# Two vector operations, four weight splits, one gate and one normalisation moved in a four-layer mixed-attention kernel

## The chip, the cores and the metric

The kernel runs on one core of one Trainium2 chip. The metric is the device time of one execution in microseconds (us), lower is better; before, it is the median of 3 runs.

## What is computed

The input is x, 512 tokens of 1024 channels in float32. Four residual layers follow each other: one of sliding-window attention (layer A), one of sparse attention with a compressed, a selected and a window branch (layer B), and two hybrid layers with three mixers side by side, a matrix LSTM, a gated linear attention and a sparse attention with top-k keys (layers C0 and C1). In short:

```python
def rms_norm(x, g):
    xf = x * lax.rsqrt(jnp.mean(x * x, axis=-1, keepdims=True) + EPS)
    return xf * g

def nsa_layer(x, norm_g, w_in, q_gain, w_out, table, k_cmp, v_cmp, k_slc, v_slc, k_win, v_win):
    proj = rms_norm(x, norm_g) @ w_in
    ...
    o_all = jnp.stack([o_cmp, o_slc, o_win], axis=2)
    o = jnp.einsum('bschd,bsch->bshd', o_all * jax.nn.silu(z), jax.nn.sigmoid(gate_logits))
    return x + o.reshape(B_, S, HQ) @ w_out

def hybrid_layer(x, norm_g, w_in, ..., w_out, rel_bias):
    p = split_columns(rmsnorm(x, norm_g) @ w_in)
    ...
    dq, dk = rmsnorm(p['dsa_q'], dsa_q_g), rmsnorm(p['dsa_k'], dsa_k_g)
    y = jnp.concatenate([y_ml, y_gla, y_dsa], axis=-1) @ w_out
    return x + y
```

So at each border between layers the new x is known only when the last output projection has been added to it, and the next layer's first product needs the norm of all 512 tokens.

## The kernel before, in words

**Layout.** x stays in SBUF as four token tiles (t = 0 to 3) of 128 tokens by 1024 channels. The normalised x is needed with channels on the partitions, so `norm_x` (L316) does for each tile: sums of squares on ScalarE (ACT, L301), a short chain of one-column VectorE (DVE) operations for the reciprocal root (L302, L139 to L149, three Newton steps of L145 and L149), the scaling `xs` on DVE in two halves of 512 channels (L326, or L328 with a gain row `E` that was fetched by the two transfers of L312), eight transposes on TensorE (PE, L331, four to a half, into a PSUM bank with the tag `t`), and `split_evac` (L359), which copies each bank out as a high part `xhi` (ACT, L361) and a rest `xlo` (DVE, L362).

**Weights.** Products keep float32 accuracy with three matmuls each: high times high (L264), rest times high (L265), high times rest (L266), or L284 to L286 with the operands swapped. `piece` (L220) streams a weight piece: a transfer from HBM into `wraw` (L228, on the queue of SyncE, SP; pieces that don't fill their tile are preceded by a memset on GpSimd, POOL, L225), the high part `whi` on ACT (L235, L242), the rest `wlo` partly on DVE (L238, L244) and partly on POOL (L249; L246 applies a gain first). The share of DVE is `dve_lo`: 0 in layer B's main part, 0.5 around its last projection, 1 in layers C. Below, mv0 is the first weight group of layer C0; its product is 96 matmuls.

**Order.** The program text gives an order, and a list scheduler with a cost model turns it once, at build time, into a fixed queue for each engine. An engine then runs its queue strictly in that order and waits at an instruction whose inputs or buffer are not ready. `s.after(a, b)` (L118) is a dependency written by hand that keeps `a` behind `b`. PSUM has 8 banks: in layer B the tags g, t, s, o have 2, 3, 2, 1 of them; in layers C 2, 2, 3, 1. Layer C's pool is opened when layer B's is closed, so its banks lie on those of layer B, in the order of first use.

**Places that matter here.** In `layer_b` the gain row `gk` is scaled on DVE (L818) and the tile `VBD` is cleared on DVE (L910). Attention is a loop over 4 head groups g and 4 token tiles t; each of the three branches (br) ends in `Block.gate` (L960): DVE writes the scaled branch `og` (L968), then POOL multiplies it by the gate `sz` (L972 for the first branch, L974 for the others) and adds it to `acc` (L975). After the third branch `to_T` (L353) transposes `acc` on PE, and `oT` goes to the output projection `out(g)`, whose sums are added to x on DVE (L586). Projections out(0) to out(2) are woven between later attention steps; out(3) stands at the end. Its last 12 matmuls, those of t = 3, need the very last gate. `layer_c` then calls `norm_x` and, in layer C0, `consts_c` (L1725), which loads and casts a mask (`gmask`, POOL, L1733) and makes small constants (DVE, L1735 to L1739). In both layers C `Dsa.early` loads two gain rows (L155) and scales one by the other on DVE (`dgk`, L1618).

Of the kernel before, what the change touches and what calls it, by code (L numbers as in the profile page):

```python
# [10 lines left out]
F32 = mybir.dt.float32  # L11
# [10 lines left out]
NT = 4  # L22
# [54 lines left out]
class Ctx:  # L77
# [281 lines left out]
    def split_evac(s, ps, hi, lo):  # L359
        nc = s.nc  # L360
        nc.scalar.activation(hi, ps, AF.Copy)  # L361
        nc.vector.tensor_tensor(lo, ps, hi.bitcast(F32), OP.subtract)  # L362

# [439 lines left out]
def layer_b(s):  # L803
    nc, tc, ia = s.nc, s.tc, s.ia
    outer = s.stack
    with ExitStack() as st:
# [3 lines left out]
        if not s.gains_known:  # L810
# [6 lines left out]
        gk = s.bcast_row(lp, ia["kv_k_gain"], 192, "gk")  # L817
        nc.vector.scalar_tensor_tensor(gk.rearrange("p (b d) -> p b d", d=64), gk.rearrange("p (b d) -> p b d", d=64), 0.125,  # L818
                                       gq[:, None, :].to_broadcast([P, 3, 64]), op0=OP.mult, op1=OP.mult)
        kvd = s.dram.tile([2, SEQ, 256], F32, name="kvd")  # L820
# [77 lines left out]
        rc = s.rstd(css, 1, 64, "rc")  # L898
        nc.vector.scalar_tensor_tensor(kc, kc, rc, gk[:, :64], op0=OP.mult, op1=OP.mult)
        s.k_pack(kc[:, None, :], kcT[:, None, :], wk, "s", "kcs")  # L900
# [3 lines left out]
        for g in range(4):  # L904
            hT4 = s.epage()[:, :256].rearrange("p (j a c) -> p j a c", j=2, a=4)
            for j in range(2):
                nc.scalar.copy(hT4[:, j], hT[:, j, None, 32 * g:32 * g + 32].to_broadcast([P, 4, 32]))
                nc.tensor.matmul(pc[:, g * 64:(g + 1) * 64], hT4[:, j].rearrange("p a c -> p (a c)"), w2t[:, j],
                                 start=j == 0, stop=j == 1)
        nc.vector.memset(VBD, 0.0)  # L910
        for j in range(4):
# [42 lines left out]
        class Block:  # L954
# [5 lines left out]
            def gate(self, po, den, br):  # L960

                g, t = self.g, self.t
                nc.vector.reciprocal(den, den)
                nc.vector.tensor_tensor(den, den, gt[:, t, br * 16 + 4 * g:br * 16 + 4 * g + 4], OP.mult)
                if br == 0 and t == 0:
                    nc.vector.memset(den[0:31], 0.0)
                og = s.opage()
                nc.vector.scalar_tensor_tensor(og.rearrange("p (h d) -> p h d", d=64), po.rearrange("p (h d) -> p h d", d=64),  # L968
                                               0.25, den[:, :, None].to_broadcast([P, 4, 64]), op0=OP.mult, op1=OP.mult)
                if br == 0:  # L970
                    self.acc = wk.tile([P, 256], F32, name="acc", tag="acc", bufs=2)
                    nc.gpsimd.tensor_tensor(self.acc, og, groups[g][1][br][t], OP.mult)  # L972
                else:
                    nc.gpsimd.tensor_tensor(og, og, groups[g][1][br][t], OP.mult)  # L974
                    nc.gpsimd.tensor_tensor(self.acc, self.acc, og, OP.add)  # L975

# [119 lines left out]

        def out(g):
            yield from s.w_out_slices(s.w(f"o{g}"), lambda k, t: (outs[g, t][:, 0, k], outs[g, t][:, 1, k]))

# [3 lines left out]
        s.pipeline(steps, fill)  # L1103
        s.dve_lo = 0.5
        for _ in out(3):
            pass
    s.stack = outer

# [84 lines left out]
def layer_c(s, L):  # L1193
    nc, tc, ia = s.nc, s.tc, s.ia
    outer = s.stack
    with ExitStack() as st:
# [5 lines left out]
        s.pens = s.pool(f"pens{L}", 3)  # L1202
        s.norm_x(ia["norm_g_2"][L])
        if L == 0:
            consts_c(s)
        k = type("K", (), {})()
# [5 lines left out]
        for e, fill in events():  # L1212
            if e in ROWS:
                tasks["m", ROWS[e]].row()
            if e[0] == "top_keys":

                s.behind = top_keys(s, k), e[1]
            elif e[0] == "keys_known":
                for _ in s.behind[0] if s.behind else []:
                    pass  # L1220
                s.behind = None
            else:
                s.weave(run(e), [(UNITS[f[0], f[1][0]], run(f)) for f in fill])
    s.stack = outer

# [380 lines left out]
class Dsa:  # L1606
# [5 lines left out]
    def early(self):  # L1612
        s, k, p = self.s, self.k, self.p
        nc, ia = s.nc, s.ia
        if p == 0:
            gq = s.bcast_row(k.lp, ia["dsa_q_g_2"][k.L], P, "dgq")
            k.dgk = s.bcast_row(k.lp, ia["dsa_k_g_2"][k.L], P, "dgk")
            nc.vector.scalar_tensor_tensor(k.dgk, k.dgk, P ** -0.5, gq, op0=OP.mult, op1=OP.mult)  # L1618
        wts = s.w(f"dq{p}")
# [167 lines left out]
```

## Time and profile before

| | |
|---|---|
| median of 3 runs | 2055.94 us (2050.4 to 2060.71) |
| profiled execution, its own time | 2054.46 us |
| profiled execution, span of the trace | 2052.7 us |
| PE busy | 1970.0 us, 96% of the span |
| DVE busy | 1415.8 us, 69% |
| ACT busy | 907.7 us, 44% |
| POOL busy | 637.6 us, 31% |
| mean granted TensorE clock | 0.990 of full speed |
| chain of work that ended last | PE 61%, DVE 15%, DMA 2%, issue 2%, ACT 2%, POOL 1% |

The span runs from the first to the last instruction; 1.76 us of the execution lie around it. PE is busy nearly always, so only those places count where PE stands or runs at half clock: what is moved elsewhere costs nothing. Times of single rows are counted from the start of the span.

### The profile page before, as it was taken

The page shows a single profiled execution, that of the slowest core. Times are in us where ns is not written, and L with a number is a line of the kernel's source. Part 1 is how long each engine was busy: PE and PEld are TensorE (multiplying, and loading weights), DVE is VectorE, ACT ScalarE, POOL GpSimd, SP SyncE. Part 2 cuts the span into 40 slices and gives each one's busy share as a digit, 9 for nine tenths or more (in the row PEclk, how much of TensorE's full clock was granted, in tenths as well). Part 3 has the DMA queues.
Part 4 walks back from the last instruction along what each step waited for, and adds up shares of the span by engine and source line. Part 5 has one row for each costly group of instructions (what it writes and reads, how often), then busy time and mean ns, then how long its engine had stood idle before and what let it go on. Part 6 is the DMA issues. An engine that isn't in the chain of part 4 may idle for free.

```text
span 2052.7 us, 29949 instructions
## 1 busy us (share of the span) xinstructions
PE 1970.0 (96%) x10139; PEld 1636.9 (80%) x10139; DVE 1415.8 (69%) x3901; ACT 907.7 (44%) x2113; POOL 637.6 (31%) x684
## 2 busy tenths in 40 slices
PE   7999989999999988999899999999999989999999
PEld 6788877788888877777778888887877778888887
DVE  6467749645656675689958775557589967965564
ACT  4355435445444553544433343434555333433432
POOL 3444325454535331015333220211013443321111
PEclk9999999999999998999999999999999999999999
DMA  5321233321121101322232232223313232332231
GB/s 178 108 82 55 82 104 108 103 83 52 55 59 60 44 9 51 109 86 72 66 103 78 74 97 87 83 78 84 108 43 99 61 94 62 95 100 84 67 107 43
DMA packets 158966, 164.93 MB, mean 80 GB/s; under 512 B 26137, under 2 KB 132560, under 8 KB 158812
## 3 DMA queue, kind: packets, MB, share of 16 engines
q1 hardware_dynamic: 158812, 163.01, 26.8%
q8 instruction: 80, 1.31, 0.3%
q14 instruction: 74, 0.61, 0.1%
HBM read 157.17 MB, written 5.80 MB: 79 GB/s over the span
## 4 chain that ended last, share of the span: by engine, by line
PE 61%; DVE 15%; DMA 2%; issue 2%; ACT 2%; POOL 1%; SPq 0%; DVEq 0%; ACTq 0%; POOLq 0%
PE b_g L264 12%; PE b_g L266 12%; PE b_g L265 12%; PE b_g L284 4%; PE b_g L285 4%; PE b_g L286 4%; DVE wlo L238 3%; PE b_o L1076 3%; PE b_s L1046 2%; DVE topw L1336 1%; PE b_t L1069 1%; PE b_s L1307 1%; DVE m L1335 1%; DVE x L586 1%; ACT whi L235 1%
## 5 line engine op out<-in xcount | busy, mean ns | idle before, releaser
L264 PE MATMUL b_g<-whi,xhi 128*128 128x512 f32 x1280 | 510.2, 399 | 21.0 <-DVE my L1525 14.2
L266 PE MATMUL b_g<-whi,xlo 128*128 128x512 f32 x1280 | 507.2, 397 | 4.2 <-DVE xlo L362 4.2
L265 PE MATMUL b_g<-wlo,xhi 128*128 128x512 f32 x1280 | 508.2, 397 | 0.1
L235 ACT ACTIVATE whi<-wraw 128x1024 fp32r<-128x1024 f32 (+2 forms) x250 | 261.0, 1047 | 181.5 <-PE b_g L266 100.0
L238 DVE TENSOR_TENSOR wlo<-wraw,whi 128x512 fp32r<-128x512 f32 (+2 forms) x376 | 268.5, 756 | 69.8 <-ACT whi L235 68.0
L264 PEld LDWEIGHTS b_g<-whi,xhi 128*128 128x128 f32 x1280 | 242.9, 190 | 75.1 <-issue 13.4
L266 PEld LDWEIGHTS b_g<-whi,xlo 128*128 128x128 f32 x1280 | 243.0, 190 | 54.4 <-DVE xlo L362 6.1
L265 PEld LDWEIGHTS b_g<-wlo,xhi 128*128 128x128 f32 x1280 | 243.1, 190 | 48.5 <-POOL wlo L249 0.9
L249 POOL TENSOR_TENSOR wlo<-wraw,whi 128x512 fp32r<-128x512 f32 (+1 forms) x138 | 182.2, 1345 | 90.7 <-ACT whi L235 81.9
L284 PE MATMUL b_g<-xhi,whi 128*128 128x512 f32 x400 | 160.7, 402 | 6.8 <-DVE x L586 4.6
L285 PE MATMUL b_g<-xlo,whi 128*128 128x512 f32 x400 | 157.9, 395 | 0.0
L286 PE MATMUL b_g<-xhi,wlo 128*128 128x512 f32 x400 | 157.6, 394 | 0.0
L586 DVE TENSOR_TENSOR x<-x,b_g 128x512 f32<-128x512 f32 x192 | 130.1, 681 | 37.4 <-PE b_g L266 36.4
L1531 POOL TENSOR_TENSOR mT<-my,mT 128x512 fp32r<-128x512 f32 x32 | 42.9, 1347 | 247.1 <-PE b_s L1307 160.3
L284 PEld LDWEIGHTS b_g<-xhi,whi 128*128 128x128 f32 x400 | 75.1, 188 | 27.1 <-DVE x L586 7.1
L1076 PEld LDWEIGHTS b_o<-v,PT 128*128 128x128 f32 x640 | 85.3, 198 | 6.3 <-DVE PT L1072 1.1
L286 PEld LDWEIGHTS b_g<-xhi,wlo 128*128 128x128 f32 x400 | 75.1, 188 | 16.4 <-issue 1.2
L285 PEld LDWEIGHTS b_g<-xlo,whi 128*128 128x128 f32 x400 | 75.2, 188 | 16.3 <-issue 1.2
L1525 DVE SCALAR_TENSOR_TENSOR my<-b_g,vec,my 128x511 f32<-128x511 f32 (+2 forms) x96 | 71.4, 744 | 23.6 <-ACT my L1522 22.4
L1076 PE MATMUL b_o<-v,PT 128*128 128x64 f32 x640 | 84.8, 275 | 1.6 <-DVE og L968 0.8
L1056 ACT ACTIVATE E<-E,nm 128x256 f32<-128x256 f32 (+1 forms) x128 | 60.9, 477 | 34.1 <-DVE nm L1055 33.5
L1049 DVE CUSTOM_DVE_ANT_0 E<-b_s,bias 128x256 f32<-128x256 f32 (+1 forms) x128 | 48.9, 385 | 37.8 <-PE b_s L1046 21.7
(413 smaller groups left out, 3971.4 us busy)
## 6 DMA issues: line engine op xcount, KB each, us to landing
wraw<-in_w_in_dram SPq DMA_DIRECT2D x240, 256.0 KB
wraw<-in_b_w_in_dram SPq DMA_DIRECT2D x64, 256.0 KB
wraw<-in_w_out_dram SPq DMA_DIRECT2D x32, 512.0 KB
wraw<-in_w_in_dram SPq DMA_DIRECT2D x24, 512.0 KB
wraw<-in_a_w_in_dram SPq DMA_DIRECT2D x32, 256.0 KB
wraw<-in_kv_w_dram SPq DMA_DIRECT2D x12, 512.0 KB
wraw<-in_a_w_out_dram SPq DMA_DIRECT2D x8, 512.0 KB
wraw<-in_b_w_out_dram SPq DMA_DIRECT2D x8, 512.0 KB
```

The source lines that it names most:

```text
L235: nc.scalar.activation(hi[:, :n, c], raw[:, :n, c], AF.Copy)
L238: nc.vector.tensor_tensor(lo[:, js, c], raw[:, js, c], hi[:, js, c].bitcast(F32), OP.subtract)
L249: nc.gpsimd.tensor_tensor(lo[:, js, c], raw[:, js, c], hi[:, js, c].bitcast(F32), OP.subtract)
L264: nc.tensor.matmul(ps[:, :width], xh, h[:, :width], start=k == 0, stop=False)
L265: nc.tensor.matmul(ps[:, :width], xh, l[:, :width], start=False, stop=False)
L266: nc.tensor.matmul(ps[:, :width], xl, h[:, :width], start=False, stop=k == n - 1)
L284: nc.tensor.matmul(ps, h[:, c * P:(c + 1) * P], s.xhi[:, k], start=k == 0, stop=False)
L285: nc.tensor.matmul(ps, h[:, c * P:(c + 1) * P], s.xlo[:, k], start=False, stop=False)
L286: nc.tensor.matmul(ps, l[:, c * P:(c + 1) * P], s.xhi[:, k], start=False, stop=k == n - 1)
L586: nc.vector.tensor_tensor(s.x[:, t, n * 512:(n + 1) * 512], s.x[:, t, n * 512:(n + 1) * 512], ps, OP.add)
L1076: nc.tensor.matmul(bl.po[:, h * 64:(h + 1) * 64], PT[:, k * P:(k + 1) * P], v[b][:, k, g * 64:(g + 1) * 64], start=k == 0, stop=k == t)
L1525: nc.vector.scalar_tensor_tensor(y[:, j:], ps[:, :SEQ - j], w, y[:, j:], op0=OP.mult, op1=OP.add)
```

## The change

1. `split_evac` remembers the last `xlo` that was written. The scaling of `gk` (layer B) and that of `dgk` (layers C) are tied behind the last `xlo` known at that point, which is the norm's last.
2. The clearing of `VBD` is tied behind the end of the compressed keys (`kc_done`).
3. Layer C0's `norm_x` is called at the end of `layer_b`, behind out(3), with layer B's PSUM pool (three banks for transposes). Its gain row comes with one transfer of 1024 channels that is issued in out(2), into a buffer of the tag `bias`, instead of two into `E` pages. `consts_c` is called later, after the event ("early", m0).
4. `dve_lo` is 1, not 0.5, for the splits that are emitted in out(3), among them those of its own later pieces and of mv0.
5. The multiplication and the addition of the last gate (g = 3, t = 3, br = 2) are on DVE, not on POOL.

```diff
     def split_evac(s, ps, hi, lo):
         nc.scalar.activation(hi, ps, AF.Copy)
-        nc.vector.tensor_tensor(lo, ps, hi.bitcast(F32), OP.subtract)
+        s.last_lo = nc.vector.tensor_tensor(lo, ps, hi.bitcast(F32), OP.subtract).ins
...
-        nc.vector.scalar_tensor_tensor(gk.rearrange("p (b d) -> p b d", d=64), gk.rearrange("p (b d) -> p b d", d=64), 0.125,
-                                       gq[:, None, :].to_broadcast([P, 3, 64]), op0=OP.mult, op1=OP.mult)
+        late = nc.vector.scalar_tensor_tensor(gk.rearrange("p (b d) -> p b d", d=64), gk.rearrange("p (b d) -> p b d", d=64), 0.125,
+                                              gq[:, None, :].to_broadcast([P, 3, 64]), op0=OP.mult, op1=OP.mult)
+        s.after(late.ins, s.last_lo)
...
-        nc.vector.scalar_tensor_tensor(kc, kc, rc, gk[:, :64], op0=OP.mult, op1=OP.mult)
+        kc_done = nc.vector.scalar_tensor_tensor(kc, kc, rc, gk[:, :64], op0=OP.mult, op1=OP.mult).ins
...
-        nc.vector.memset(VBD, 0.0)
+        s.after(nc.vector.memset(VBD, 0.0).ins, kc_done)
...
-                    nc.gpsimd.tensor_tensor(og, og, groups[g][1][br][t], OP.mult)
-                    nc.gpsimd.tensor_tensor(self.acc, self.acc, og, OP.add)
+                    eng = nc.vector if (g, t, br) == (3, NT - 1, 2) else nc.gpsimd
+                    eng.tensor_tensor(og, og, groups[g][1][br][t], OP.mult)
+                    eng.tensor_tensor(self.acc, self.acc, og, OP.add)
...
         def out(g):
+            if g == 2:
+
+                row = wk.tile([P, D], F32, name="gain", tag="bias", bufs=2)
+                nc.sync.dma_start(row, bass.AP(tensor=ia["norm_g_2"].tensor, offset=ia["norm_g_2"][0].offset, ap=[[0, P], [1, D]]))
+                s.rows = [row[:, :512], row[:, 512:]]
...
         s.pipeline(steps, fill)
-        s.dve_lo = 0.5
+        s.dve_lo = 1
         for _ in out(3):
             pass
+        s.norm_x(ia["norm_g_2"][0])
...
-        s.norm_x(ia["norm_g_2"][L])
-        if L == 0:
-            consts_c(s)
+        if L:
+            s.norm_x(ia["norm_g_2"][L])
...
+            if e == ("early", ("m", 0)) and L == 0:
+                consts_c(s)
...
-            nc.vector.scalar_tensor_tensor(k.dgk, k.dgk, P ** -0.5, gq, op0=OP.mult, op1=OP.mult)
+            late = nc.vector.scalar_tensor_tensor(k.dgk, k.dgk, P ** -0.5, gq, op0=OP.mult, op1=OP.mult)
+            s.after(late.ins, s.last_lo)
```

What this moves in the engines' queues, at the places that the prediction speaks of:

DVE's queue at the border from layer A to layer B, before (-) and after (+), where `rr` and `rt` are the one-column tiles of the norm of token tile 2 and `xlo` is that of tile 0:

```order
-L910 MEMSET VBD 128x1024
 L142 TENSOR_SCALAR rr<-rv 128x1
 L244 SCALAR_TENSOR_TENSOR wlo<-wraw,gains,whi 128x512
-L818 SCALAR_TENSOR_TENSOR gk<-gk,gq 128x192
-L145 SCALAR_TENSOR_TENSOR rt<-rr,rh 128x1
-L362 TENSOR_TENSOR xlo<-b_t,xhi 128x4x128 x2
-L149 SCALAR_TENSOR_TENSOR rr<-rt,rr 128x1
-L145 SCALAR_TENSOR_TENSOR rt<-rr,rh 128x1
-L149 SCALAR_TENSOR_TENSOR rr<-rt,rr 128x1
+L145 SCALAR_TENSOR_TENSOR rt<-rr,rh 128x1
+L149 SCALAR_TENSOR_TENSOR rr<-rt,rr 128x1
+L145 SCALAR_TENSOR_TENSOR rt<-rr,rh 128x1
```

The memset and the scaling of `gk` leave this place (`gk` now stands behind the norm's last `xlo`, `VBD` far behind), and L149 and a second L145 come ahead of the first `xlo`.

POOL's queue in layer B's last quarter, before, where L225 clears a `wraw` tile and L249 are splits of out(3)'s and mv0's weights:

```order
L975 TENSOR_TENSOR acc<-acc,og 128x256
L249 TENSOR_TENSOR wlo<-wraw,whi 128x512
L225 MEMSET wraw 128x4x128
L249 TENSOR_TENSOR wlo<-wraw,whi 128x512
L974 TENSOR_TENSOR og<-og,sz 128x256
L225 MEMSET wraw 128x4x128
L972 TENSOR_TENSOR acc<-og,sz 128x256
L975 TENSOR_TENSOR acc<-acc,og 128x256
```

and after (the gate's lines L972, L974 and L975 are L973, L976 and L977 there):

```order
L977 TENSOR_TENSOR acc<-acc,og 128x256
L225 MEMSET wraw 128x4x128
L976 TENSOR_TENSOR og<-og,sz 128x256
L977 TENSOR_TENSOR acc<-acc,og 128x256
L225 MEMSET wraw 128x4x128
L973 TENSOR_TENSOR acc<-og,sz 128x256
L473 TENSOR_TENSOR qd<-qr,rr 128x512
```

The two splits have left POOL, and the addition stands directly behind the multiplication.

PE's queue at the border from layer B to layer C0, before, from the last three of out(3)'s 12 matmuls on:

```order
L264 MATMUL b_g<-whi,oT 128x512
L265 MATMUL b_g<-wlo,oT 128x512
L266 MATMUL b_g<-whi,oT 128x512
L331 MATMUL b_t<-ident,xs 128x128 x8
L264 MATMUL b_g<-whi,xhi 128x512
L265 MATMUL b_g<-wlo,xhi 128x512
L331 MATMUL b_t<-ident,xs 128x128 x4
L266 MATMUL b_g<-whi,xlo 128x512
```

and after:

```order
L264 MATMUL b_g<-whi,oT 128x512
L265 MATMUL b_g<-wlo,oT 128x512
L266 MATMUL b_g<-whi,oT 128x512
L331 MATMUL b_t<-ident,xs 128x128 x24
L264 MATMUL b_g<-whi,xhi 128x512
L265 MATMUL b_g<-wlo,xhi 128x512
L266 MATMUL b_g<-whi,xlo 128x512
```

The transposes of token tile 0 have gone ahead of the 12 matmuls; the 24 of tiles 1, 2 and 3 stand in one piece ahead of mv0's first matmul, where before they lay in groups of four among its first 50. DVE's queue there, after, between the last gate and the first `xlo`:

```order
L969 SCALAR_TENSOR_TENSOR og<-b_o,sm 128x256
L1254 MEMSET wa 128x256
L976 TENSOR_TENSOR og<-og,sz 128x256
L1745 MEMSET heads_9281 128x2
L1749 MEMSET ones 128x1
L977 TENSOR_TENSOR acc<-acc,og 128x256
L1746 MEMSET heads_9281 64x1
L1747 MEMSET heads_9281 64x1
L362 TENSOR_TENSOR oT<-b_t,oT 128x256
L362 TENSOR_TENSOR xlo<-b_t,xhi 128x4x128 x2
```

The gate's two operations stand where POOL's were waited for, with small memsets between, and the scalings `xs` of tiles 0 and 1, which stood around the last gate before, are further up.

## Rows read from the trace of the kernel before

**Rows 1.** The page, busy time, share and instructions of each engine.

```profile
PE 1970.0 (96%) x10139; PEld 1636.9 (80%) x10139; DVE 1415.8 (69%) x3901; ACT 907.7 (44%) x2113; POOL 637.6 (31%) x684
```

**Rows 2.** Timeline of PE, border A to B: start, duration, instruction, [idle before <-releaser].

```profile
261.82 0.80 PE L266 MATMUL b_g<-whi,xlo 128*128 128x512 f32 x1 [3.22 <-DVE xlo L362]
262.41 0.63 PE L264 MATMUL b_g<-whi,xhi 128*128 128x512 f32 x1
...
267.11 0.51 PE L266 MATMUL b_g<-whi,xlo 128*128 128x512 f32 x1
```

**Rows 3.** Timeline of DVE, border A to B.

```profile
256.95 0.91 DVE L910 MEMSET VBD<- 128x1024 f32 x1 [0.16 <-issue]
...
258.84 1.19 DVE L818 SCALAR_TENSOR_TENSOR gk<-gk,gq 128x192 f32<-128x192 f32 x1
259.95 1.22 DVE L145 SCALAR_TENSOR_TENSOR rt<-rr,rh 128x1 f32<-128x1 f32 x1
261.09 1.28 DVE L362 TENSOR_TENSOR xlo<-b_t,xhi 128x512 fp32r<-128x512 f32 x2
...
262.47 0.22 DVE L145 SCALAR_TENSOR_TENSOR rt<-rr,rh 128x1 f32<-128x1 f32 x1
```

**Rows 4.** Timeline of POOL, border A to B.

```profile
258.32 1.49 POOL L246 TENSOR_TENSOR wraw<-wraw,gains 128x512 f32<-128x512 f32 x1
259.89 1.26 POOL L249 TENSOR_TENSOR wlo<-wraw,whi 128x512 fp32r<-128x512 f32 x1
```

**Rows 5.** Timeline of POOL, layer B's last quarter.

```profile
727.17 1.27 POOL L249 TENSOR_TENSOR wlo<-wraw,whi 128x512 fp32r<-128x512 f32 x1
728.39 1.17 POOL L974 TENSOR_TENSOR og<-og,sz 128x256 f32<-128x256 f32 x1
...
730.67 0.72 POOL L975 TENSOR_TENSOR acc<-acc,og 128x256 f32<-128x256 f32 x1
```

**Rows 6.** Timeline of PE, layer B's last quarter, border to C0, one row of C0.

```profile
731.45 0.65 PE L353 MATMUL b_t<-ident,acc 128*128 128x128 f32 x2 [2.64 <-POOL acc L975]
...
778.91 1.60 PE L1076 MATMUL b_o<-v,PT 128*128 128x64 f32 x8 [0.84 <-DVE og L968]
...
780.73 5.22 PE L1076 MATMUL b_o<-v,PT 128*128 128x64 f32 x24
789.44 0.69 PE L353 MATMUL b_t<-ident,acc 128*128 128x128 f32 x2 [3.48 <-POOL acc L975]
...
795.89 1.29 PE L331 MATMUL b_t<-ident,xs 128*128 128x128 f32 x8
797.43 0.53 PE L264 MATMUL b_g<-whi,xhi 128*128 128x512 f32 x1 [0.25 <-ACT xhi L361]
...
801.85 0.60 PE L331 MATMUL b_t<-ident,xs 128*128 128x128 f32 x4
...
1032.82 0.47 PE L264 MATMUL b_g<-whi,xhi 128*128 128x512 f32 x1 [1.75 <-DVE my L1525]
```

**Rows 7.** Windows: PE, PEld, DVE, ACT, POOL busy, granted clock, DMA, GB/s.

```profile
730.00:735.00 5.00, 3.55 (x14) 3.15 (x15) 2.43 (x9) 1.58 (x5) 1.39 (x3) 0.66 0.50 47
...
780.00:785.00 5.00, 5.00 (x26) 5.00 (x25) 3.02 (x14) 0.58 (x1) 0.80 (x1) 0.50 0.03 10
```

**Rows 8.** Timeline of DVE, layer B's last quarter and the border to C0.

```profile
727.41 0.41 DVE L968 SCALAR_TENSOR_TENSOR og<-b_o,sm 128x256 f32<-128x256 f32 x1
...
786.07 0.42 DVE L968 SCALAR_TENSOR_TENSOR og<-b_o,sm 128x256 f32<-128x256 f32 x1 [1.78 <-PE b_o L1076]
...
796.79 1.17 DVE L238 TENSOR_TENSOR wlo<-wraw,whi 128x256 fp32r<-128x256 f32 x2
...
804.34 0.16 DVE L302 TENSOR_TENSOR ss<-ss 128x1 f32<-128x1 f32 x1 [0.45 <-ACT sq L301]
...
806.26 1.42 DVE L328 SCALAR_TENSOR_TENSOR xs<-x,rr,E 128x512 f32<-128x512 f32 x2
```

**Rows 9.** Timeline of DVE, border C0 to C1.

```profile
1405.11 0.29 DVE L1618 SCALAR_TENSOR_TENSOR dgk<-dgk,dgq 128x128 f32<-128x128 f32 x1 [1.70 <-DMA dgk<-in_dsa_k_g_dram]
```

## The prediction

> **What bounds the kernel now.** I read the page first: PE is busy for 96% of the span, DVE for 69%, POOL for 31% [rows 1]. So a change pays only where PE stands, or where its clock is halved. I then listed PE's idle spells of over 1 us and found that the change touches five places with one. At the border from layer A to layer B PE waits 3.22 us for the first `xlo`, and the 12 matmuls behind it, from 262.41 to 267.11, start 0.427 us apart (4.70 / 11) [rows 2]. In layer B's last quarter it waits 2.64 us for a gate on POOL [rows 6], in a stretch with a granted clock of 0.66 [rows 7]. Before the last attention products it waits 0.84 us for DVE's `og` [rows 6], which stands in DVE's queue behind an `xs` that waits for the gain row's transfer. Behind them it waits 3.48 us for the last gate [rows 6]. At the border from C0 to C1 DVE waits 1.70 us for `dgk`'s row [rows 9]. The reader is to see in each place which wait ends last, and what is queued behind it.
>
> **Clock.** PE's granted clock shows two levels, 1.2 and 2.4 GHz. At the lower one a 512-column matmul follows the last after 0.427 us [rows 2], at the full one after about half of that: each in a half-clock stretch costs 0.2 us more. From 780 to 785 the level is the lower one though PE is busy throughout [rows 7].
>
> **Part by part** (minus is faster)
>
> 1. *Memset and `gk`, border A to B.* Their durations are 0.91 and 1.19 us, and the first `xlo` stands behind them [rows 3]. Taking both out gives -2.1, and L149 and a second L145, which now stand ahead of `xlo`, give back about twice the 0.22 of a free L145: -1.7. If the wait shrinks that far, the half clock behind it may go too, 12 x 0.2 = 2.4; that would make -4.1. But the rows say more. `gk`'s operation ends at 260.03, 0.22 behind the end of POOL's L246 (258.32 + 1.49 = 259.81), and a one-column L145 takes 1.22 us at 259.95 and ends at 261.17, just behind POOL's L249 (259.89 + 1.26 = 261.15) [rows 3, 4], where a similar L145 takes 0.22 with POOL idle [rows 3]. So such an operation of DVE, with two SBUF inputs, waits out the POOL operation under way, and then POOL takes the next turn. Ahead of `xlo` stood three operations with two SBUF inputs in this stretch (L244, `gk`, L145); now there are four (L244, L145, L149, L145). POOL's three operations run to about 261.2 as before, one DVE operation between any two of them, and then an L149 or an L145 is still to come. The first `xlo` then starts at about 261.5, not at 261.09. I take **+0.4**, since two rows of DVE end with POOL's; the bounds are -4.1 and +0.7. `gk` and `VBD` land where DVE has slack; without that cover they cost 2.1.
>
>    The Trainium skill, page "SBUF — State Buffer", section "Who interferes with whom", says that a VectorE instruction with two SBUF inputs and a GpSimd instruction that reads SBUF exclude each other for their whole length. This case's trace agrees (1.22 us for an L145 beside POOL, 0.22 without). By that rule this term is +0.4; by the removed durations alone it would be -4.1.
>
> 2. *Splits off POOL, layer B's last quarter.* The L249 of 727.17 runs until 728.44, and the gate's L974 behind it takes 1.17 us [rows 5] where the free L975 of the same size takes 0.72 [rows 5]; a second `wraw` memset and a first-branch product stand between it and its addition. `og` is ready at 727.82 [rows 8]. Without the L249 the product starts some 0.6 earlier and is 0.45 shorter, and the addition follows at once instead of 1.1 later: -2.1. DVE runs the two splits now, 0.7 us each, and one can lie ahead of `og`: +0.5. **-1.6**, between 0 and -2.6. PE's wait falls from 2.64 to about 1, and an idle spell of 1.75 us is followed by a matmul of 0.47 us, the full clock's length [rows 6]. At 0.66 in a 5 us window [rows 7] about 3.4 us ran at half clock, which costs half of that: **-1.7**, between 0 and -1.7.
>
> 3. *Gain row early.* DVE no longer stands for the row ahead of `og` at 778, and the two `xs` are further up. PE's 0.84 us wait there goes: **-0.8** (0 to -1.2). The 24 matmuls from 780.73 take 5.22 us at half clock [rows 6, 7]. With a denser PE before them the full clock may hold; that is worth up to half of 5.22, and as much again in out(3)'s 12 matmuls (2.4). I take the first alone and not in full: **-2.2** (0 to -4.6).
>
> 4. *Last gate on DVE.* From the start of `og` (786.07) to the transposes (789.44) pass 3.37 us [rows 6, 8]. On DVE it is three operations of 128x256, 0.42 each by `og`'s row [rows 8], a memset of a similar size and some small ones, about 1.6 in all: **-1.7**. The mask's cast on POOL could lie beside the product and hold it for 1 us: -0.7 to -2.0.
>
> 5. *The norm ahead of mv0.* Before, mv0's first matmul starts 1.54 us after the end of out(3) (795.89 to 797.43), and six groups of four transposes lie among its matmuls, 0.60 us each [rows 6], some 0.36 net of the overlap with their neighbours: 2.2 in all. Now all 24 stand ahead of mv0. Moreover mv0's first accumulator lies on a bank that was a transpose bank in layer B, so it also waits for the `xlo` of tile 3's first half. DVE's queue from the end of out(3), with 0.64 to 0.71 for a 128x512 operation [rows 3, 8]: result latency 0.2, the last L586 0.7, two L238 1.4, two half ones 1.1 [rows 8], `xlo` of tile 1 1.3, `xs` of tile 2 1.4, tile 3's root 1.9 (804.34 to 806.26 [rows 8]) with the `xlo` of tile 2 in between 1.3, tile 3's first `xs` 0.7. That is 10.0. Then its transposes and `xhi`, 1.2, and its `xlo`, 0.7: 12.0. So 12.0 - 1.5 - 2.2 = **+8.3**. Bounds: +5 where `xlo` and splits fit into the root's gaps, +10.5 where the transposes gave nothing back. PE then comes out of some 10 us with 24 transposes as its only work, and I expect one half-clock stretch as behind the other waits: **+1.7** (0 to +3.4).
>
> 6. *`dgk` behind the norm, border C0 to C1.* PE's wait there ends with a chain of DVE behind `dgk`. I take two thirds of the 1.70, since PE still ran under the start of it: **-1.1** (0 to -1.7) [rows 9]. At layer C0 it hid behind out(3): 0.
>
> 7. *The rest.* Four more L238 on DVE (0.7 each), the later constants and the reshuffled queues of layers B and C: 0, covered by DVE's 31% of idle time and by the weight buffers ahead of PE; without that cover up to +2.8.
>
> Sum: +0.4 - 1.6 - 1.7 - 0.8 - 2.2 - 1.7 + 8.3 + 1.7 - 1.1 = +1.3. On the profiled execution's 2054.5 that is **2055.8**; this execution is 1.5 below the median of its runs, so against the median nothing changes.
>
> **Rivals**
>
> - *POOL doesn't hold DVE at the border A to B* (DVE's short operations slip in between): term 1 is -4.1. For it: POOL's turns leave 0.08 us between them. Against: those two rows. 2055.8 - 4.5 = 2051.3.
> - *mv0 doesn't wait for the whole norm* (the banks or DVE's order let it start behind tile 0, and the rest hides): term 5 is -3.7 (1.5 and 2.2 saved) and its clock cost 0, and the full clock also holds through out(3), -2.4. That is 2055.8 - 8.3 - 3.7 - 1.7 - 2.4 = 2039.7; with half of term 5's swing 2046. For it: the sums of tiles 0 and 1 are long done. Against: the 24 transposes in one piece, in order.
> - *The stall decides*, slower: the same wait at the price of +10.5 with two half-clock stretches behind it (+3.4), while the half clock at 731 and 780 stays (terms of -1.7 and -2.2 become 0). 2055.8 + 2.2 + 1.7 + 3.9 = 2063.6; with terms 2 and 4 at their lower ends 2066. It decides from a stall of about 11 us on (+9 net), where the gains of all the other parts are used up. For it: every step of that chain is on one engine, in order. Against: at two places PE's idle spell shrinks to a length that was followed by the full clock at 1032.
> - *Nothing comes of it*: DVE takes as long for the gates and splits as POOL did, and the norm is as late as before; 2054.5. It shares the forecast's range.
>
> **Numbers.** Forecast and "nothing" 0.44, POOL not holding 0.18, mv0 free 0.18, stall 0.20. The forecast's own range is 2048 to 2062. The range to hold it 8 times in 10 takes in the first rival, half of the second and most of the third: 2044 to 2065. A measurement can tell about 0.5% (10.3 us) from no change, so faster means below 2045.7 and slower above 2066.2. Faster: most of "mv0 free" and the low end of the first rival, 0.17. Slower: half of the stall's cases and a rest, 0.12. Same: 0.71.
>
> **What would show it.** In the profile after: an L145 or L149 of over 1 us ahead of the first `xlo` near 260, and that `xlo` at its old distance from out's last matmul (by the rival, two small ones and PE's wait under 2 us); at 730 no L249 on POOL and a wait of about 1 us for the gate; near 788 a gate wait of under 2 us, released by DVE; then out(3), and some 10 us in which PE does 24 transposes, with the first mv0 matmul released by DVE's `xlo` and a half clock behind it; near 1405 no wait for `dgk`. The prediction is wrong if that stall is under 5 us or over 15, or if any place outside these five moves by more than 3 us.

## The result and the profile after

| | before | after |
|---|---|---|
| median of 7 runs each | 2055.94 us (2050.40 to 2060.71) | 2069.61 us (2059.73 to 2070.75) |
| profiled execution, its own time | 2054.46 us | 2059.73 us |
| span of the trace | 2052.7 us | 2057.9 us |
| mean granted TensorE clock | 0.990 | 0.989 |

The ratio is 1.0053, 95% interval 1.0033 to 1.0072: slower, by about half a per cent. In a second comparison, with 12 runs of it and 35 of before on one chip (e1 below), it is 1.0034 (1.0020 to 1.0048), 2067.87 against 2059.63 us. I had forecast 2055.8 in a range of 2044 to 2065, and "no difference" as the likeliest; 2069.61 lies outside.

The profiled execution of after is the shortest of its seven runs, at clock 0.989; the other six have 0.984 to 0.987 and 2067.8 to 2070.8 us. So the trace shows 5.3 us of a loss that is 8 us (e1) to 14 us (medians above). First where the 5.3 lie. The table cuts both traces at the same instructions of PE and gives the time from each to the next:

| stretch, up to the start of | before | after | difference |
|---|---|---|---|
| layer B's first transposes (L331) | 255.75 | 255.00 | -0.75 |
| the first matmul with `xlo` | 6.07 | 5.95 | -0.1 |
| the transposes of the first gate (L353) | 181.12 | 181.03 | -0.1 |
| the gate near 731 | 288.51 | 288.75 | +0.2 |
| the next gate | 15.86 | 16.17 | +0.3 |
| the next gate | 18.29 | 20.24 | **+2.0** |
| the last gate | 23.84 | 18.46 | **-5.4** |
| mv0's first matmul | 7.99 | 17.75 | **+9.8** |
| what follows mv0 | 25.39 | 24.77 | -0.6 |
| C0's second run of `goT` matmuls | 325.64 | 324.51 | -1.1 |
| C0's first `moT` matmul | 64.07 | 66.18 | **+2.1** |
| the `doT` matmul behind C0's last `og` transposes | 186.87 | 187.38 | +0.5 |
| C1's first transposes | 23.42 | 22.06 | -1.4 |
| C1's second run of `goT` matmuls | 354.39 | 352.43 | -2.0 |
| C1's first `moT` matmul | 64.10 | 66.17 | **+2.1** |
| the last matmul | 206.61 | 206.41 | -0.2 |

`goT`, `moT` and `doT` are the transposed outputs of the gated linear attention, the matrix LSTM and the sparse attention, as they go into the output projection of a layer C. The marked stretches carry the difference: one loss, one gain, one new wait, and the same small loss once in each layer C.

**The loss.** PE's timeline after, from the last gate on (start, duration, instruction, idle before and its releaser):

```profile
785.60 0.63 PE L353 MATMUL b_t<-ident,acc 128*128 128x128 f32 x2 [1.75 <-DVE heads L1747]
...
790.90 0.40 PE L266 MATMUL b_g<-whi,oT 128*128 128x512 f32 x1
791.13 1.03 PE L331 MATMUL b_t<-ident,xs 128*128 128x128 f32 x8
796.29 1.94 PE L331 MATMUL b_t<-ident,xs 128*128 128x128 f32 x8 [4.13 <-DVE xs L328]
800.85 1.94 PE L331 MATMUL b_t<-ident,xs 128*128 128x128 f32 x8 [2.62 <-DVE xs L328]
803.35 0.79 PE L264 MATMUL b_g<-whi,xhi 128*128 128x512 f32 x1 [0.56 <-DVE xlo L362]
```

The last gate comes after 1.75 us, not 3.48 [rows 6]. But mv0 starts 12.45 us after the start of out(3)'s last matmul (790.90 to 803.35); from the end of out(3), where the next transposes begin, it is 12.22 (791.13 to 803.35), and before it was 1.54 [rows 6]. In between PE does 24 transposes and waits for DVE. DVE's timeline of the same time, the main steps:

```profile
792.01 1.62 DVE L238 TENSOR_TENSOR wlo<-wraw,whi 128x512 fp32r<-128x512 f32 x3
...
794.01 1.28 DVE L362 TENSOR_TENSOR xlo<-b_t,xhi 128x512 fp32r<-128x512 f32 x2
...
795.40 1.41 DVE L328 SCALAR_TENSOR_TENSOR xs<-x,rr,gain 128x512 f32<-128x512 f32 x2
...
799.95 1.42 DVE L328 SCALAR_TENSOR_TENSOR xs<-x,rr,gain 128x512 f32<-128x512 f32 x2
802.60 0.69 DVE L362 TENSOR_TENSOR xlo<-b_t,xhi 128x512 fp32r<-128x512 f32 x1 [1.23 <-ACT xhi L361]
```

DVE is busy nearly throughout at first (4.93 of 5 us from 792), PE hardly (0.87 us), and its clock falls to the half one, which mv0 then begins with (columns: PE, PEld, DVE, ACT, POOL busy, granted clock, DMA share, GB/s):

```profile
792.00:797.00 5.00, 0.87 (x6) 0.74 (x5) 4.93 (x15) 2.16 (x6) 0.00 (x0) 0.89 0.50 159
...
802.00:807.00 5.00, 4.44 (x13) 3.27 (x12) 1.38 (x2) 1.16 (x2) 0.00 (x0) 0.50 0.01 3
```

**The gain and the new wait.** PE's timeline after, layer B's last attention steps, and DVE's ahead of the new wait:

```profile
763.79 0.88 PE L1078 MATMUL b_o<-v,PT 128*128 128x64 f32 x6 [2.10 <-DVE PT L1074]
...
781.80 2.05 PE L1078 MATMUL b_o<-v,PT 128*128 128x64 f32 x16
```

```profile
761.18 1.41 DVE L328 SCALAR_TENSOR_TENSOR xs<-x,rr,gain 128x512 f32<-128x512 f32 x2
...
763.18 0.55 DVE L1074 COPY PT<-b_t 128x384 f32<-128x384 f32 x1
```

The last attention products run at the full clock now (16 in 2.05 us, where 24 took 5.22 [rows 6]) and the 0.84 us ahead of them is gone. For that, token tile 1's scaling, which has its gain row early, stands in DVE's queue ahead of the copy `PT` that PE needs: PE waits 2.10 us there, and before no idle spell of over 1 us was there.

**The border A to B** is as it was. After, PE and DVE, then POOL:

```profile
260.95 0.80 PE L266 MATMUL b_g<-whi,xlo 128*128 128x512 f32 x1 [3.10 <-DVE xlo L362]
```

```profile
256.73 1.23 DVE L145 SCALAR_TENSOR_TENSOR rt<-rr,rh 128x1 f32<-128x1 f32 x1
258.00 0.96 DVE L149 SCALAR_TENSOR_TENSOR rr<-rt,rr 128x1 f32<-128x1 f32 x1
258.99 1.30 DVE L145 SCALAR_TENSOR_TENSOR rt<-rr,rh 128x1 f32<-128x1 f32 x1
260.22 0.68 DVE L362 TENSOR_TENSOR xlo<-b_t,xhi 128x512 fp32r<-128x512 f32 x1
```

```profile
256.33 1.61 POOL L249 TENSOR_TENSOR wlo<-wraw,whi 128x512 fp32r<-128x512 f32 x1
257.90 1.04 POOL L246 TENSOR_TENSOR wraw<-wraw,gains 128x512 f32<-128x512 f32 x1
259.02 1.26 POOL L249 TENSOR_TENSOR wlo<-wraw,whi 128x512 fp32r<-128x512 f32 x1
```

The memset and `gk` are gone, and three one-column steps have taken their time: each ends just behind a POOL operation (257.96 behind 257.94, 258.96 behind 258.94, 260.29 behind 260.28). `xlo` starts 5.22 us after the transposes of 255.00; before it was 5.34 (255.75 to 261.09). These steps belong to token tile 1; my sentence ahead of the first fence on DVE's queue had called them tile 2's.

**The gate near 731** waits 1.00 us, not 2.64:

```profile
730.73 0.45 PE L353 MATMUL b_t<-ident,acc 128*128 128x128 f32 x2 [1.00 <-POOL acc L977]
```

**The border C0 to C1.** Before, PE waited twice behind the layer's last `og` transposes, the second time for the chain behind `dgk`; after, only the first of the two waits is left. PE before, then after:

```profile
1399.40 0.50 PE L264 MATMUL b_g<-whi,doT 128*128 128x512 f32 x1 [1.17 <-DVE x L586]
...
1406.22 0.47 PE L264 MATMUL b_g<-whi,doT 128*128 128x512 f32 x1 [1.09 <-DVE rr L149]
```

```profile
1406.19 0.50 PE L264 MATMUL b_g<-whi,doT 128*128 128x512 f32 x1 [0.95 <-DVE x L586]
```

**What the tie of `dgk` did inside the layers C.** I had said that the tie holds `dgk` behind the norm's last `xlo`. It doesn't: `split_evac` remembers every split, also those of the transposed outputs, and when `dgk` is emitted the last one is a `goT`. So `dgk` runs at 1149.24 instead of 794.35, directly behind `goT`'s last split, and the same way in C1 (1777.29 instead of 1405.11). The first product that needs it, POOL's `dqk<-dqk,dgk`, starts at 1149.60 instead of 1137.34. PE from `goT`'s matmuls to the first `moT` one, before and after:

```profile
1148.46 0.40 PE L264 MATMUL b_g<-whi,goT 128*128 128x512 f32 x1
...
1212.53 0.39 PE L264 MATMUL b_g<-whi,moT 128*128 128x512 f32 x1
```

```profile
1152.63 0.39 PE L264 MATMUL b_g<-whi,goT 128*128 128x512 f32 x1
...
1167.89 0.50 PE L264 MATMUL b_g<-whi,goT 128*128 128x512 f32 x1 [1.18 <-DVE x L586]
...
1218.81 0.40 PE L264 MATMUL b_g<-whi,moT 128*128 128x512 f32 x1
```

and DVE and POOL after:

```profile
1148.91 0.42 DVE L362 TENSOR_TENSOR goT<-b_t,goT 128x256 fp32r<-128x256 f32 x1
1149.24 0.28 DVE L1627 SCALAR_TENSOR_TENSOR dgk<-dgk,dgq 128x128 f32<-128x128 f32 x1
...
1165.60 1.12 DVE L147 TENSOR_TENSOR rt<-rr 128x4 f32<-128x4 f32 x1
```

```profile
1165.42 1.27 POOL L1693 TENSOR_TENSOR dpb<-dbias,pen 128x512 f32<-128x512 f32 x1 [2.46 <-issue]
```

A step of four columns that takes 0.16 us elsewhere ends here with a POOL operation (1166.72 behind 1166.69), and PE waits 1.18 us for the L586 behind it. From `goT`'s second run to the first `moT` it takes 66.18 us, and 64.07 before. The same stretch is 66.14 to 66.18 us in both layers C of all ten runs that have the ties (the change, e1, e3 to e6, e8, e10 to e12), and 64.07 to 64.10 in the four without them (before, e2, e7, e9). So the ties cost 2.1 us in each layer C, 4.2 in all, for the 1.4 us that they gain at the border. That it is `dgk`'s tie is argued: it is the only tied operation in these layers.

### The profile page after: what moved, and what is told of

It reads as the page before. It is cut to its first block, busy times and chain, and to the rows that moved or that the text cites. A ratio compares the mean times of both kernels' runs of the same rounds, so it can differ in the third digit from the quotient of the medians.

```text
span 2057.9 us, 29960 instructions
## 1 busy us (share of the span) xinstructions
PE 1972.1 (96%) x10139; PEld 1638.3 (80%) x10139; DVE 1423.1 (69%) x3907; ACT 908.2 (44%) x2113; POOL 632.0 (31%) x678
## 4 chain that ended last, share of the span: by engine, by line
PE 59%; DVE 16%; DMA 3%; issue 2%; ACT 2%; POOL 1%; SPq 0%; DVEq 0%; ACTq 0%; POOLq 0%
PE b_g L264 11%; PE b_g L266 11%; PE b_g L265 11%; PE b_g L284 4%; PE b_g L285 4%; PE b_g L286 4%; DVE wlo L238 3%; PE b_o L1078 3%; PE b_s L1048 2%; PE b_t L1071 1%; DVE topw L1345 1%; PE b_s L1316 1%; DVE m L1344 1%; ACT whi L235 1%; DVE x L586 1%
## 5 line engine op out<-in xcount | busy, mean ns | idle before, releaser
L249 POOL TENSOR_TENSOR wlo<-wraw,whi 128x512 fp32r<-128x512 f32 (+1 forms) x134 | 176.0, 1339 | 75.2 <-ACT whi L235 70.2
L586 DVE TENSOR_TENSOR x<-x,b_g 128x512 f32<-128x512 f32 x192 | 130.2, 681 | 37.3 <-PE b_g L266 36.2
L1598 POOL TENSOR_TENSOR mtho<-mtho,mgain 128x256 f32<-128x256 f32 x32 | 23.9, 745 | 155.3 <-DVE mtho L1597 115.2
```

The costliest lines, as they stand in the source:

```text
L249: nc.gpsimd.tensor_tensor(lo[:, js, c], raw[:, js, c], hi[:, js, c].bitcast(F32), OP.subtract)
L586: nc.vector.tensor_tensor(s.x[:, t, n * 512:(n + 1) * 512], s.x[:, t, n * 512:(n + 1) * 512], ps, OP.add)
```

## The experiments

All were timed beside runs of before on the same chip; the ratio is to those.

| run | what | median us | before us | ratio, 95% interval |
|---|---|---|---|---|
| e1 | the change again | 2067.87 | 2059.63 | 1.0034 (1.0020 to 1.0048) |
| e2 | before + norm moved | 2067.28 | 2059.63 | 1.0027 (1.0012 to 1.0042) |
| e3 | the change, norm not moved | 2059.44 | 2059.63 | 1.0001 (0.9984 to 1.0019) |
| e4 | the change, other PSUM banks | 2067.54 | 2059.63 | 1.0035 (1.0019 to 1.0051) |
| e5 | the change, late tiles' transposes in C0 | 2056.72 | 2058.14 | 0.9994 (0.9979 to 1.0009) |
| e6 | before + ties + `xlo` first | 2053.87 | 2058.14 | 0.9973 (0.9959 to 0.9987) |
| e7 | before + gate on DVE, scalings behind it | 2054.71 | 2058.14 | 0.9980 (0.9964 to 0.9996) |
| e8 | e6 and e7 together | 2051.43 | 2058.14 | 0.9963 (0.9945 to 0.9981) |
| e9 | before + splits on DVE | 2057.56 | 2060.13 | 0.9981 (0.9968 to 0.9994) |
| e10 | before + the three ties | 2060.14 | 2060.13 | 1.0006 (0.9995 to 1.0017) |
| e11 | e8 + splits on DVE | 2051.31 | 2059.94 | 0.9953 (0.9937 to 0.9969) |
| e12 | e8 again | 2053.81 | 2059.94 | 0.9972 (0.9961 to 0.9984) |

**e1, the change once more.** No edit.

> The change as it stands, once more, for a second profile of it. Its seven runs lie at 2067.8 to 2070.8 us but for the profiled one, 2059.7. Theory S (the norm's stall ahead of mv0 sets the loss, half-clock stretches come on top): median 2064 to 2070, and where a run is 8 to 10 us longer than the profile already read, the extra is half-clock stretches (granted clock 0.985 instead of 0.989), each 3.4 us long and worth 1.7 us, not longer waits. Rival D (some wait differs from run to run, a late transfer for instance): same clock, a wait of several us that the first profile doesn't have.

Measured: 2063.66 to 2074.07 us. The profiled run has clock 0.983 and a span of 2069.3 us, 11.4 longer than the first trace of the same kernel. Most of the difference stands already by layer B's first transposes (261.37 after the start, not 255.00), in a part that the change doesn't touch. Windows over the same stretch of the first trace of the change, then of e1:

```profile
85.00:112.00 27.00, 25.38 (x118) 18.90 (x117) 6.59 (x22) 8.47 (x19) 12.70 (x12) 0.94 0.52 157
```

```profile
85.00:112.00 27.00, 27.00 (x94) 19.17 (x92) 2.92 (x6) 4.89 (x6) 10.57 (x9) 0.68 0.50 151
```

PE is busy for all of 27 us and does 94 matmuls instead of 118. So far theory S holds, and D falls: the runs of one kernel differ by half-clock time, not by a new wait in this stretch. The 35 runs of before show the same, from 2053.61 us at clock 0.992 to 2071.84 at 0.982. It explains little of the loss, though: the median clock of the change is 0.986 here, that of before 0.987, and 0.001 of 2060 us is about 2 of the 8 us (an estimate).

**e2, part 3 alone.** Before, with these lines:

```diff
+                row = wk.tile([P, D], F32, name="gain", tag="bias", bufs=2)
...
+        s.norm_x(ia["norm_g_2"][0])
...
-        s.norm_x(ia["norm_g_2"][L])
-        if L == 0:
-            consts_c(s)
+        if L:
+            s.norm_x(ia["norm_g_2"][L])
```

> Before, with part 3 alone (C0's norm in layer B, its row early, the constants later). Theory S: this part alone makes the kernel slower, first mv0 matmul about 12 us after out(3)'s last one, 2060 to 2068 us (+8 net of the transposes, +2 to +4 of half clock). Rival M (the loss comes from the moved splits, the gate on DVE or the ties): 2050 to 2057 us.

Measured: +7.65 us, inside S's range; M falls as the main cause. mv0 starts 14.7 us after the start of out(3)'s last matmul (794.22 to 808.90), where S had said about 12, and 19.7 us after the last gate's transposes (17.75 with the gate on DVE, 7.99 before):

```profile
802.76 1.94 PE L331 MATMUL b_t<-ident,xs 128*128 128x128 f32 x8 [7.27 <-DVE xs L328]
```

**e3, all but part 3.** The change without the lines of e2.

> The change without part 3: the ties, the splits on DVE and the gate on DVE stay, the norm stands in layer C0 as before. Theory S: 2048 to 2054 us, faster than before by the gate's and the quarter's waits (1.7 + 1.6) and some half clock. Rival M: 2060 to 2070 us, the loss is still there.

Measured: 2059.44, the time of before. The loss is gone with the norm's move, but the gain that S expected of the rest isn't there. PE's timeline gives one reason, at the gate:

```profile
791.08 1.10 PE L1078 MATMUL b_o<-v,PT 128*128 128x64 f32 x8 [1.16 <-DVE og L969]
...
792.38 5.22 PE L1078 MATMUL b_o<-v,PT 128*128 128x64 f32 x24
800.59 0.66 PE L353 MATMUL b_t<-ident,acc 128*128 128x128 f32 x2 [2.98 <-DVE heads L1740]
```

and DVE's:

```profile
798.35 0.42 DVE L976 TENSOR_TENSOR og<-og,sz 128x256 f32<-128x256 f32 x1
798.70 0.74 DVE L328 SCALAR_TENSOR_TENSOR xs<-x,rr,E 128x512 f32<-128x512 f32 x1
...
800.03 0.41 DVE L977 TENSOR_TENSOR acc<-acc,og 128x256 f32<-128x256 f32 x1
```

Two scalings of the next layer stand between the gate's product and its addition, 1.3 us; the other wait is 1.16 us (0.84 before), and the 24 products take 5.22 us at half clock, as before. What the gate wins on DVE it loses to its neighbours in the queue. The second reason is in the layers C: the ties, which e3 keeps, cost the 4.2 us above and gain 1.4.

**e4, other banks.** In `layer_c`:

```diff
         s.banks(f"ps_c{L}", 2, 3)
+        if L == 0:
+            s.bk("s")
```

> The change, with the s banks of layer C0's PSUM pool laid out first, so that mv0's first accumulator no longer lies on a transpose bank of layer B and waits for xhi of tile 0 alone. The 24 transposes still stand in one piece ahead of it in PE's queue. Theory S1 (the bank's wait for the last xlo is the price): 1.3 us less stall, from the end of the last transposes on only, since PE's queue holds the transposes ahead. Theory S2 (the queue of PE is the price, in-order transposes that wait for DVE): time within 3 us of the change, stall of 10 instead of 12 us. If the bank alone were the price, 8 us would come back and the time would be 2060.

Measured: the loss of the change to 0.0001. PE's timeline, from the last transposes on:

```profile
803.66 1.94 PE L331 MATMUL b_t<-ident,xs 128*128 128x128 f32 x8 [2.61 <-DVE xs L328]
805.26 0.78 PE L264 MATMUL b_g<-whi,xhi 128*128 128x512 f32 x1
```

mv0 starts 1.60 us after those transposes and without a wait, where the change took 2.50 (800.85 to 803.35), of it 0.56 waiting for `xlo`. So the bank is 0.9 us of the stall, and the time doesn't show it. The queue is the price: S2.

**e5, the late tiles' transposes in C0.** The scalings stay in layer B and are kept (tile 3's in two `PT` buffers):

```diff
+                if cut and t > 1:
+                    s.cut.append((t, h, xs))
+                else:
+                    s.turn(t, h, xs)
...
         if L:
             s.norm_x(ia["norm_g_2"][L])
+        else:
+            for a in s.cut:
+                s.turn(*a)
```

`turn` is the old end of `norm_x`'s loop (transposes and `split_evac`).

> The change, but the transposes and copies of C0's token tiles 2 and 3 stand in layer C0 (its PSUM pool); the sums and scalings of all tiles and the whole of tiles 0 and 1 stay in layer B. PE's queue then has 16 transposes ahead of mv0, those of tile 2 behind its first 24 matmuls and those of tile 3 behind the next. Theory S2 (PE's in-order queue holds mv0 behind transposes that wait for DVE's scaling of tiles 2 and 3): first mv0 matmul 4 to 6 us after out(3)'s last one instead of 12.45, time 6 to 9 us below the change, 2058 to 2062. Rival (DVE's chain is the bound, whatever PE's order): PE waits for tile 2 and 3 inside mv0 instead, time within 3 us of the change, 2065 to 2070.

Measured: 2056.72, below the 2058 to 2062 that S2 gave. On its own chip that is 1.4 us below before, with an interval that takes in no difference; the change (e1) was 8.2 above before on its chip. PE's timeline:

```profile
793.04 1.04 PE L340 MATMUL b_t<-ident,xs 128*128 128x128 f32 x8
796.66 0.50 PE L264 MATMUL b_g<-whi,xhi 128*128 128x512 f32 x1 [2.58 <-DVE xlo L371]
...
803.40 1.03 PE L340 MATMUL b_t<-ident,xs 128*128 128x128 f32 x8
...
809.74 1.03 PE L340 MATMUL b_t<-ident,PT 128*128 128x128 f32 x8
```

mv0 starts about 4 us behind out(3), and the transposes of tiles 2 and 3 lie inside mv0 without a wait, though DVE's queue is the same up to tile 2's scaling. So neither DVE's work nor the early row made the loss, but PE's order: 16 transposes whose inputs come late, ahead of matmuls that don't need them. mv0's 96 matmuls are four groups of 24, one for each token tile, and the first two groups need only tiles 0 and 1.

**e6, `xlo` first.** Before with the three ties, and in the Newton steps of layer B's tile 1:

```diff
+                step = nc.vector.scalar_tensor_tensor(t, y, h, y, op0=OP.mult, op1=OP.mult)
+                if s.hold is not None:
+                    s.after(step.ins, s.hold)
```

where `s.hold` is tile 0's last `xlo`.

> Before, with the ties of gk, VBD and dgk, and at the border from A to B token tile 1's first Newton step tied behind tile 0's last xlo, so that no one-column step stands ahead of it. Theory L (DVE's steps with two SBUF inputs wait out POOL's operations, xlo with one PSUM input does not): xlo starts at once behind the second L244, about 2.5 us after the first transposes instead of 5.3; PE's wait of 3.2 falls below 1; the steps of over 1 us stand behind xlo; time 2 to 5 us below before, with the half-clock stretch there gone. Rival W (tile 1 is late then): PE waits ahead of the next 12 transposes, and the time is that of before within 2 us.

Measured: 0.9973, theory L. DVE's timeline:

```profile
259.48 1.29 DVE L367 TENSOR_TENSOR xlo<-b_t,xhi 128x512 fp32r<-128x512 f32 x2 [0.29 <-ACT xhi L366]
...
261.58 1.14 DVE L145 SCALAR_TENSOR_TENSOR rt<-rr,rh 128x1 f32<-128x1 f32 x1
```

`xlo` starts 2.1 us after the transposes of 257.38 and takes its usual 0.65 us each beside POOL; the stretched steps stand behind it. PE has no wait of over 0.25 us for it or for tile 1 behind it, so W falls, and no half clock follows (granted 1.00 from 255 to 275). The ties alone (e10) gave nothing.

**e7, the gate and its neighbours.** Part 5, and:

```diff
+                    ins = nc.vector.scalar_tensor_tensor(xs, xt, r, rows[h], op0=OP.mult, op1=OP.mult).ins
+                    if s.last_gate is not None:
+                        s.after(ins, s.last_gate)
```

> Before, with the last gate on DVE and C0's scalings of tiles 0 and 1 tied behind its addition (norm and gain rows otherwise as before). Theory G (in the run without the norm's move the gate gained little because two scalings, 1.3 us, lay between its product and its addition, and og stood behind a scaling that waits for the gain row): wait for the last gate 1.7 to 1.9 us instead of 3.5, no wait of 0.84 ahead of the last attention products, 3 to 6 us below before with half clock. Rival (the half clock there comes from the attention's own short matmuls): the waits shrink, the time by 2 us at most.

Measured: -3.4 us of median, interval -7.4 to -0.8: theory G. The wait is that of the change, now without the norm's move, and `og` waits for PE alone:

```profile
783.22 2.05 PE L1079 MATMUL b_o<-v,PT 128*128 128x64 f32 x16
787.01 0.66 PE L355 MATMUL b_t<-ident,acc 128*128 128x128 f32 x2 [1.75 <-DVE acc L978]
```

**e8 and e12, both.** The edits of e6 and e7.

> Both together: the ties, xlo first, the gate on DVE with the scalings behind it. The two places are 500 us apart, so the gains add: 5 to 10 us below before, ratio 0.995 to 0.9975. If half-clock stretches elsewhere decide the level, the ratio is 1.000 within 0.002 though both waits are shorter in the trace.

> e8 once more, as the neighbour of the run above: ratio 0.9945 to 0.998.

Measured: 0.9963 and 0.9972; the gains add, about 6 us. Both still have the 2.1 us in each layer C that the ties cost.

**e9, the splits alone.** `s.dve_lo = 1` ahead of out(3).

> Before, with part 4 alone (the share of DVE is 1 for the splits emitted in out(3)). My forecast's step: the gate's wait near 731 falls from 2.64 to about 1 us and no half clock follows it, 3.3 us below before. Rival Q (DVE's two 128x512 splits stand ahead of og and of the row maxima, so what PE waits for comes later by as much): the gate's wait is shorter, but PE reaches the transposes at the same time from out(2)'s start on, the half-clock stretch stays, and the time is that of before within 2 us.

Measured: 0.9981, 2.6 us by the medians, interval 1.2 to 6.6: my own step, and Q falls for this kernel. From the first gate to that near 731 it takes 286.82 us, 1.7 less than before, and no half clock follows.

**e10, the ties alone.** Parts 1 and 2.

> Before, with the three ties alone (gk, VBD, dgk). By my forecast: first xlo as late as before (POOL's three operations hold the one-column steps), 0.4 us slower there, 1.1 faster at the border C0 to C1: 1 us below before at most. Rival N (the removed durations count): 3 to 5 us below, PE's wait of 3.2 at 1.5. Rival R (at the border C0 to C1 another DVE operation takes dgk's place): PE's wait of 1.09 there stays within 0.2.

Measured: 1.0006. The wait for `xlo` is the change's. At C1's border the matmul that waited 1.09 us for `dgk`'s chain before doesn't wait, so R falls (the wait of 1.05 at 1401.93 is the one for L586 that before has at 1399.40):

```profile
263.37 0.80 PE L266 MATMUL b_g<-whi,xlo 128*128 128x512 f32 x1 [3.10 <-DVE xlo L362]
...
1401.93 0.50 PE L264 MATMUL b_g<-whi,doT 128*128 128x512 f32 x1 [1.05 <-DVE x L586]
...
1407.51 0.39 PE L264 MATMUL b_g<-whi,doT 128*128 128x512 f32 x1
```

From the first of these `doT` matmuls to C1's first transposes all ten runs with the ties take 22.03 to 22.10 us, and the four without 23.00 to 23.86: the gain at the border is real, 1.4 us in this trace, and the 4.2 us inside the layers C use it up.

**e11, e8 with the splits.**

> e8 with the splits of out(3) on DVE too (part 4, which gave 0.9981 alone). If the places are independent, 0.9963 x 0.9981 = 0.9944, about 3 us below e8. If DVE's extra splits take back what the gate's wait gives once the order is another, the same as e8 within 2 us.

Measured: 0.9953, against 0.9972 for e8 on the same chip; the intervals overlap, so that the splits add something here isn't shown. It is the fastest version found, some 9 us below before, and by the two ratios (0.9953 and 1.0034, on different chips) some 17 below the change.

## Why the prediction was wrong

- **Step 1, border A to B (+0.4): right**, -0.1, and for its reason: DVE's one-column steps wait out POOL's operations. e6 shows it from the other side: with `xlo`, which reads PSUM and one SBUF tile, ahead of them, the wait is gone. The Trainium skill, page "SBUF — State Buffer", section "Who interferes with whom", says the same, that an instruction of VectorE with at most one SBUF input (outside its two-port modes) does not contend with GpSimd; the trace of e6 agrees (`xlo` 1.29 us for two beside POOL, L145 1.14).
- **Step 5, the norm ahead of mv0 (+8.3, clock +1.7): right.** The sum was 12.0 us from out(3)'s end (its terms add to 11.9), and 12.2 came; less the 1.54 of before and the 0.62 that mv0's matmuls gave back, that is +10.1 where 10.0 was forecast with the clock. e2 shows that this part alone makes the loss, and e5 that PE's order is why. One reason was off: I named the bank as well, and it is 0.9 us (e4).
- **Steps 3 and 4, the gate and the half clock ahead of it (-0.8, -2.2, -1.7): right in the trace**, -5.4 for -4.7. But the half sentence in 3, "the two `xs` are further up", was priced at nothing, and they stand in front of DVE's copy for PE, +2.0.
- **Step 2, the splits (-1.6 and, for the clock, -1.7): the first half right, the second wrong.** The gate's wait shrank as forecast, to 1.00. The stretch up to there, from the first gate on, is 288.5 us in before, e2 and e7 and 286.8 with the splits alone (e9), 290.2 with the ties and no splits (e6, e8, e12; e10 has 291.9, with a half-clock stretch in it) and 288.6 to 288.8 with both (the change, e1, e3 to e5, e11): the splits give 1.6 to 1.7 with or without the ties. The table's +0.2 hides it for two reasons. With the ties the first gate stands 10 matmuls earlier in PE's queue (873 instead of 883 behind layer B's first transposes), so that those 10 now lie in this stretch. And PE runs part of the way up to the first gate at half clock after (0.86 granted from 348 to 360, 1.00 before); e7, with before's queue up to there, has the same 0.86. The half clock behind the gate near 731 stayed: 0.66 granted from 730 to 735 in both traces. For the -1.7 the stretch behind that gate has +0.3. With the splits alone it went (e9, 1.00 from 729 to 745); why it stayed in the change is open.
- **Step 6, `dgk` (-1.1): right at its place, and wrong at layer C0, which it put at 0.** At the border the wait is gone, -1.4. But the tie, behind `goT`'s split and not behind the norm's, costs 2.1 us in each layer C.
- **The step that failed** is the term that 3, 6 and 7 put at nothing: what the moved work does where it lands. Step 7 said that the reshuffled queues are "covered by DVE's 31% of idle time". The trace shows +2.0 at the copy `PT` and +4.2 behind the moved `dgk`, in places where PE waits for DVE at that moment; DVE's share of the whole says nothing of them. For the same reason my sentence that what is moved elsewhere costs nothing doesn't hold. Beside it stands the half clock of step 2, -1.7, which stayed.
- **The sum.** The trace's steps give +5.3 for my +1.3, 4.0 more: +2.0 from the new wait; +3.7 from the stretches that end with the first gate, with that near 731 and with the one behind it, where I had -3.3 (the splits' 1.6 came, the half clock behind the gate stayed, and the one near 352 stands against them); +1.1 from the layers C, which come out at 0.0 where I had -1.1 (the ties' 4.2 against -1.4 at the border and -2.8 in the rest, of which -2.0 ahead of C1's `goT`, where before has a half-clock stretch, 0.83 granted from 1585 to 1595, and after none, 1.00 from 1589 to 1599); less 2.8 in small ones, the start, the border A to B, the gate and the norm. The other part of the error is the scale: I set the sum on one execution 1.5 us below its median and held that the distance stays. After, the profiled execution is 9.9 below the median, for its half-clock time (e1). Even with the right sum, the forecast would have been 2060, and the median of that comparison 10 us above it. In the larger comparison the change costs 8.2 us by the medians, in which the trace's 5.3 fit with some 3 us left to the clock and to scatter; which of the two is open.

Of the rivals, "the stall decides" had the right direction, and I gave it 0.20, but not for its reasons: the stall cost what the forecast itself had summed, not +10.5 with two half-clock stretches, and the half clock at 780 went. What used up the gains were the new wait and the ties.

## What to carry to other kernels

Before a chain is moved ahead of a big product, look at PE's queue rather than at the text: an in-order engine waits at the first instruction with a late input, and 16 late transposes ahead of ready matmuls cost more than every wait that the move took away; moved back among the matmuls (e5) they cost nothing. An operation that no one waits for is dangerous where it stands between two that someone waits for: tying the scalings behind the gate (e7) and the one-column steps behind `xlo` (e6) gave what moving the work between engines had not. A tie should be read in the trace at the place where the operation lands: `dgk`, tied behind the wrong split, took away a wait at one border and cost three times as much further on. And a sum of gains should name, for each wait removed, the next thing in the same queue.

## What the runs showed beside it

Two traces of the same program differ by 11.4 us, 6.4 of them in the first 260 us. There lies a stretch in which PE was busy throughout and had much less of the full clock in one trace than in the other (0.68 granted from 85 to 112, against 0.94). Over 35 runs of before the time goes from 2053.61 to 2071.84 us as the granted clock goes from 0.992 to 0.982. Half-clock time at a place that the change doesn't touch can thus move a run by more than any step of this change but the norm's.
